# Reordering the dense jobs under the FoX attention, with an even fill and operands kept as 512-token tiles

## The chip, the cores and the metric

The kernel runs on one core of a Trainium2 chip. Its time is device microseconds, the median of the runs shown. The core has a matrix engine (PE, with its weight loads as a second row, PEld), three engines for elementwise work (VectorE, in the profile DVE; ScalarE, ACT; GpSimd, POOL) and a queue that starts transfers (SP). Each engine works through its own list of instructions in order; semaphores make one wait for another.

## The reference

One layer of a decoder trunk over 1024 tokens and 1024 channels, all in fp32. After an RMS norm, one input projection feeds eight HGRN heads and sixteen FoX heads; both groups are gated, concatenated, projected back and added to the residual. Then a per-layer embedding is gated in, and a final norm ends it.

```python
u = rmsnorm(h, norm_w[i])
proj = jnp.einsum('bsd,de->bse', u, w_in[i])
hq, hf, hi, hg, fq, fk, fv, fg, fz = jnp.split(proj, SPLIT_POINTS, axis=-1)
y_h = hgrn2_branch(hq, hf, hi, lb_all[i], hgrn_gn[i]) * jax.nn.silu(hg)
y_f = fox_branch(fq, fk, fv, fz, fox_fb[i]) * jax.nn.silu(fg)
y = jnp.concatenate([y_h, y_f], axis=-1)
h = h + jnp.einsum('bse,ed->bsd', y, w_out[i])
ple = jnp.einsum('bsk,kd->bsd', p[i], w_ple[i])
h = h + jax.nn.sigmoid(jnp.einsum('bsd,de->bse', h, w_ple_gate[i])) * ple
...
# fox_branch, per head: causal softmax of
logits = (jnp.einsum('bhtd,bhsd->bhts', qb, kb).astype(f32) * scale
          + F[:, :, q0:q1, None] - F[:, :, None, :q1])
```

## The kernel before

**Dense products.** Tokens lie along the free axis. A dense product multiplies eight 128x128 weight tiles with the normed input u. Both are split into a high and a low part (`split`, L80 and L81), and three products of parts are summed: per 128 output channels and 512 tokens that is 8 x 3 = 24 matmuls into one PSUM tile `ps`, of which there are two ("proj", pool `pp`). A dense *job* (`dense_steps`) is two such groups, 48 matmuls. u is eight tiles of 1024 tokens, high and low, each read in halves.

**FoX.** The 16 heads are worked in eight pairs. A pair p needs four jobs: q (`fox_q`), k (`fox_k`), v (`fox_v`) and a gate (`fox_gate`). Once a k or q half is out of PSUM, GpSimd makes a copy with the heads' halves swapped (`swap`, L442). For v, ScalarE copies a half to `vt` (L478), four PE transposes turn it (L483), ScalarE copies that to `v` (L485) and GpSimd swaps it. A gate writes `sg` through ScalarE (tanh, L433) and VectorE (L434); there is a single `sg` buffer and a single output buffer `o`, beside `o7` for the last pair.

A pair has four chunks: head i = 0, 1, and within it first the later 512 tokens (c = 1, wide rows of logits, 512 down to 288), then the earlier (c = 0, narrow, 256 down to 32). While a chunk is finished, the logits of the following one are begun. `Chunk.mix` does that in two parts. In each part stand 16 logit matmuls of the following chunk (L809; VectorE adds the bias and takes the extremum, L823), the exponentials of this chunk (ScalarE L845, then VectorE transposes L846), and a *fill*: `ahead.fill(FOX_FILL[p])` draws that many columns of dense work from a list of jobs, in steps of one 512-column matmul. After both parts come the maxima `mxo` (VectorE L832, L833) and the values matmuls `po` (L857), whose halves are added through `avt` (ScalarE L868) into `o` (VectorE L869). With c = 0 the row sums are turned on PE (L898), taken out by ScalarE and VectorE (`zk` L902, `zt` L903), inverted, and sent through DRAM (`zd`) to come back as `rz`, broadcast.

**What sets the order.** PE's instructions are pinned to the order in which the Python code issues them. The other engines are ordered by a list scheduler. The dense jobs issued during pair p are, before the change, v, q and k of pair p+1 and then (p from 1 to 5) the gate of p; the last pair does the gates of 6 and 7. Ahead of a pair's last chunk `until(("k", p + 1))` draws jobs until k of the next pair is done, because that chunk issues the next pair's first logits. What a job leaves to be done later (the turning of v, the row sums) is put on a list `pending` that is emptied at the third step of each group of 24 (`flush`), and at a pair's end. If a fill ends on a group's last matmul, what follows that group (its copy out of PSUM) is issued only when the next fill, or the final draining, resumes the job.

**End of FoX.** `finish` multiplies `o` by `rz` (GpSimd L916) and by `sg` (L918) and stores it. The HGRN outputs are loaded again (`y_load`: two into slots of `k`, two into `v`, four into the probabilities' tile `pt1` near the end), split into `y_h`, which takes the memory of u, and multiplied by the first half of the output weights (L96 to L98); `ev_h1` (L1000) adds the result to x.

## Time and profile before

| | |
|---|---|
| median of 3 runs | 1357.4 us (1357.19 to 1359.22) |
| the profiled execution's own time | 1359.17 us |
| its span, first to last instruction | 1357.1 us |
| PE busy | 1286.0 us (95%) |
| VectorE, ScalarE, GpSimd busy | 789.4, 473.9, 355.2 us |
| FoX, first logits to the first product with `y_h` | 548.4 to 1068.2 us |

The profiled execution has 2.1 us around its span. In the views quoted below a line of a timeline gives start, duration, engine, line, operation and, in brackets, how long the engine stood idle before it and what released it. A line of a wait view gives the waiting engine and line, what it waited for, total us, number of times and the longest. A line of a table by stage gives the stretch, its length, the busy time of PE, PEld, DVE, ACT and POOL with instruction counts, the granted PE clock, and the transfers' share and rate. A busy PE is not a PE at full speed: logits that are spaced out by a slow reader still count as busy.

### The profile page before, as it was taken

Reading aid. Unit: us, or ns where it says so; the run is one execution under the profiler, and the core shown is the slowest. Engines: PE = TensorE matmul, PEld = TensorE weight load, DVE = VectorE, ACT = ScalarE, POOL = GpSimd, SP = SyncE. Lnnn points to the kernel's source line nnn. Section 1 sums busy time; section 2 is a strip of 40 time slices with the busy share of each in tenths; the row PEclk is TensorE's granted clock in tenths of the full one; section 3 lists DMA queues with packets and bytes.
Section 4 is the critical chain, followed back from the end, with each engine's and each line's share of the span. In section 5 each row is a group of like instructions: output and inputs, shape, how many; then the busy total and the mean of one; then the engine's idle time right before and its main releaser. Section 6 shows DMA issues by size and latency. Waiting matters only on the chain. (4 is left out here: it accounts for less than half of the span.)

```text
span 1357.1 us, 26771 instructions
## 1 busy us (share of the span) xinstructions
PE 1286.0 (95%) x10996; PEld 1022.7 (75%) x10996; DVE 789.4 (58%) x1988; ACT 473.9 (35%) x1144; POOL 355.2 (26%) x288
## 2 busy tenths in 40 slices
PE   6899999999999999999999999999987899999996
PEld 4787888888888878665676767676654688888895
DVE  6746575656746574567665656565758623333465
ACT  6413122221312233443443444444434511212455
POOL 3613123112211123333332324242330300101232
PEclk9999999999999999998999999999998999999998
DMA  7312111101101012111221212121221453212312
GB/s 281 131 43 63 48 37 59 63 17 63 48 32 63 19 48 80 48 56 58 68 72 55 71 56 72 55 71 56 71 87 49 163 193 109 86 47 70 132 63 78
DMA packets 38682, 101.17 MB, mean 75 GB/s; under 512 B 6688, under 2 KB 8864, under 8 KB 38560
## 3 DMA queue, kind: packets, MB, share of 16 engines
q1 hardware_dynamic: 38416, 98.95, 22.1%
q8 instruction: 86, 1.41, 0.4%
q0 software_dynamic: 144, 0.52, 0.1%
q14 instruction: 36, 0.29, 0.1%
HBM read 82.54 MB, written 16.91 MB: 73 GB/s over the span
## 5 line engine op out<-in xcount | busy, mean ns | idle before, releaser
L356 PE MATMUL ps<-ulo,whi 128*128 128x512 f32 x896 | 359.7, 401 | 0.0
L356 PE MATMUL ps<-uhi,whi 128*128 128x512 f32 x896 | 356.8, 398 | 0.0
L356 PE MATMUL ps<-uhi,wlo 128*128 128x512 f32 x896 | 354.6, 396 | 0.0
L81 POOL TENSOR_TENSOR wlo<-wf,whi 128x1024 fp32r<-128x1024 f32 x59 | 144.7, 2453 | 496.4 <-ACT whi L80 468.1
L356 PEld LDWEIGHTS ps<-ulo,whi 128*128 128x128 f32 x896 | 169.3, 189 | 51.6 <-issue 17.6
L356 PEld LDWEIGHTS ps<-uhi,whi 128*128 128x128 f32 x896 | 169.3, 189 | 42.3 <-issue 7.4
L356 PEld LDWEIGHTS ps<-uhi,wlo 128*128 128x128 f32 x896 | 169.5, 189 | 34.8 <-issue 1.6
L845 ACT ACTIVATE x<-x,mxo 128x512 f32<-128x512 f32 (+15 forms) x256 | 130.4, 511 | 72.1 <-DVE mxo L833 72.1
L80 ACT CAST whi<-wf 128x1024 fp32r<-128x1024 f32 (+1 forms) x77 | 79.6, 1035 | 213.8 <-PE ps L97 92.5
L823 DVE CUSTOM_DVE_ANT_0 x<-lg,fb 128x512 f32<-128x512 f32 (+15 forms) x256 | 101.8, 431 | 90.2 <-PE lg L809 83.4
L846 DVE STREAM_TRANSPOSE pt<-x 128x512 f32<-128x512 f32 (+15 forms) x256 | 115.9, 459 | 40.8 <-ACT x L845 36.5
L809 PE MATMUL lg<-k,qx 64*32 64x512 f32 (+15 forms) x1024 | 83.5, 431 | 24.7 <-POOL k L442 20.3
L96 PE MATMUL ps<-yhi,whi 128*128 128x512 f32 x256 | 100.8, 394 | 5.5 <-DVE h L1000 5.5
L97 PE MATMUL ps<-ylo,whi 128*128 128x512 f32 x256 | 100.8, 394 | 0.0
L98 PE MATMUL ps<-yhi,wlo 128*128 128x512 f32 x256 | 100.6, 393 | 0.0
L809 PE MATMUL lg<-k,q 64*32 64x480 f32 (+15 forms) x1024 | 82.9, 429 | 3.8 <-DVE mx L823 3.8
L857 PEld LDWEIGHTS po<-pt,v 64*64 64x64 f32 x1536 | 53.6, 133 | 23.4 <-issue 9.4
L857 PE MATMUL po<-pt,v 64*64 64x256 f32 (+7 forms) x1536 | 69.4, 320 | 0.0
L809 PEld LDWEIGHTS lg<-k,qx 64*32 64x32 f32 x1024 | 28.9, 109 | 45.7 <-POOL k L442 22.3
L96 PEld LDWEIGHTS ps<-yhi,whi 128*128 128x128 f32 x256 | 48.7, 190 | 15.9 <-issue 5.9
L97 PEld LDWEIGHTS ps<-ylo,whi 128*128 128x128 f32 x256 | 48.8, 191 | 10.5 <-DVE ylo L81 0.2
L98 PEld LDWEIGHTS ps<-yhi,wlo 128*128 128x128 f32 x256 | 48.8, 191 | 10.3
(204 smaller groups left out, 2178.8 us busy)
## 6 DMA issues: line engine op xcount, KB each, us to landing
wf<-in_w_in_dram SPq DMA_DIRECT2D x64, 512.0 KB, 3.5
fb<-fd SPq DMA_DIRECT2D x64, 128.0 KB, 3.3
wf<-in_w_out_dram SPq DMA_DIRECT2D x16, 512.0 KB, 3.5
yf<-yd SPq DMA_DIRECT2D x16, 512.0 KB, 4.9
x<-in_xT_dram SPq DMA_DIRECT2D x8, 512.0 KB, 9.2
pled<-pleo SPq DMA_DIRECT2D x16, 256.0 KB, 3.1
yd<-sg SPq DMA_DIRECT2D x8, 512.0 KB, 2.6
rz<-zd SPq DMA_DIRECT2D x16, 256.0 KB, 3.4
```

Source lines behind the costliest of these rows:

```text
L80: pin(nc.scalar.copy(hi, src))
L81: pin(lo_engine.tensor_tensor(out=lo, in0=src, in1=hi, op=ALU.subtract))
L96: pin(mm(ps, whi, uhi, start=i == 0, stop=False))
L97: pin(mm(ps, whi, ulo, start=False, stop=False))
L98: pin(mm(ps, wlo, uhi, start=False, stop=i == n - 1))
L356: pe(mm(ps, x, y, start=i == j == 0, stop=i == n - 1 and j == 2))
L809: mm(ps[32 * j : 32 * j + 32, m % 2, : 32 * n], q[:, 32 * (j // 2) :][:, :32], k[not own][rows].rearrange("p (t a k) -> p t a k", a=2, k=3 ...
L823: nc.vector.tensor_tensor_reduce(out=x, in0=ps[:, m % 2, : 32 * n], in1=copies[m % 2][:, : 32 * n], scale=1.0, scalar=BIG, op0=ALU.add, op ...
L845: nc.scalar.activation(x, x, AF.Exp, bias=self.other[:, g : g + 1], scale=-1.0, accum_out=zs[:, m : m + 1])
L846: nc.vector.transpose(self.probs[:, : m + 1, g], x.rearrange("p (t k) -> p t k", k=32))
L857: mm(po[half[t % 2], r, 32 * first : 256], v_t[self.p][half[r], t ^ r, half[self.i]], self.probs[half[r], t, first:].rearrange("p g q -> p ...
```

## The change

Four things are done together.

1. **Order of jobs.** During pair p the jobs are now k and q of pair p+1, the gate of p (p from 1 to 4), then v of pair p+1. The weight loads (`w_in_loads`) follow that order.
2. **A gate moves.** The gate of pair 5 is no longer computed in pair 5 but at the beginning of the last pair, which then has three gates (5, 6, 7). Since `o` is needed by pair 6, the output of pair 5 is stored after its multiplication by `rz`, loaded again in the last pair as `olate` (into a `k` slot), multiplied by the gate and stored again. One of the early `y_load`s goes to a slot of `q` instead.
3. **Even fill.** FOX_FILL becomes exact multiples of 18 matmuls (9216 columns) or 24 (12288): 18 x 8 = 144 is three jobs, 24 x 8 = 192 is four. The last pair's fill goes from 8 matmuls to 18 in each part.
4. **512-token tiles.** u, `y_h` and `hm` become separate tiles for each half of the tokens, so that a half's memory is free as soon as that half has been read.

```diff
-FOX_FILL = (9200, 12300, 12300, 12300, 12300, 12300, 9200, 4000)
+FOX_FILL = (9216, 12288, 12288, 12288, 12288, 9216, 9216, 9216)
+FIRST_LATE = PAIRS_F - 3
...
-    upool = ctx.enter_context(tc.tile_pool(name="u", bufs=2 * KT))
+    upool = ctx.enter_context(tc.tile_pool(name="u", bufs=2 * KT * NCH))
...
+    def operands(*names):
+        return [[tuple(upool.tile([P, CH], F32R, name=name, tag="u") for name in names) for _ in range(KT)] for _ in range(NCH)]
...
         for p in range(PAIRS_F - 1):
-            tiles += [T_FV + p + 1, T_FQ + p + 1, T_FK + p + 1] + ([T_FG + p] if 0 < p < PAIRS_F - 2 else [])
-        tiles += [T_FG + PAIRS_F - 2, T_FG + PAIRS_F - 1]
+            tiles += [T_FK + p + 1, T_FQ + p + 1] + ([T_FG + p] if 0 < p < FIRST_LATE else []) + [T_FV + p + 1]
+        tiles += [T_FG + p for p in range(FIRST_LATE, PAIRS_F)]
...
-                    ahead.fill(FOX_FILL[self.p] if following else 5000)
+                    ahead.fill(FOX_FILL[self.p])
...
-                    ahead.jobs += [gate_late(p - 1), fox_gate(p)]
-                    for x in ((fp, "k", 4), (fp, "k", 4), (fp, "v", 2, 2)):
+                    y_t[FIRST_LATE] = fp.tile([P, S], F32, name="olate", tag="k", bufs=4)
+                    nc.sync.dma_start(out=y_t[FIRST_LATE], in_=yd[KT + FIRST_LATE])
+                    ahead.jobs += [gate_late(p - 2), gate_late(p - 1), fox_gate(p)]
+                    for x in ((fp, "k", 4), (fi, "q", 2), (fp, "v", 2, 2)):
                         y_load(*x)
...
-                    ahead.jobs += [fox_v(p + 1), fox_q(p + 1), fox_k(p + 1)]
-                    if 0 < p < PAIRS_F - 2:
+                    ahead.jobs += [fox_k(p + 1), fox_q(p + 1)]
+                    if 0 < p < FIRST_LATE:
                         ahead.jobs.append(fox_gate(p))
+                    ahead.jobs.append(fox_v(p + 1))
...
                 finish(p, False)
-                if p != PAIRS_F - 2:
+                if p == FIRST_LATE:
+                    nc.sync.dma_start(out=yd[KT + p], in_=y_t[p])
+                elif p != PAIRS_F - 2:
                     finish(p, True)
...
-        y_h = [(upool.tile([P, S], F32R, name="yhi", tag="u"), upool.tile([P, S], F32R, name="ylo", tag="u")) for _ in range(KT)]
+        y_h = operands("yhi", "ylo")
```

PE, near the end of pair 3, where its second head's row sums are turned (`zs`). Before, with gate matmuls around:

```order
L356 MATMUL ps<-uhi,wlo 128x512
L356 MATMUL ps<-uhi,whi 128x512
L898 MATMUL ps<-cst,zs 16x128
L356 MATMUL ps<-ulo,whi 128x512
L356 MATMUL ps<-uhi,wlo 128x512
```

Now, with matmuls of v of pair 4 around, and the turning of that v's first half (`vt`) right behind:

```order
L359 MATMUL ps<-uhi,wlo 128x512
L359 MATMUL ps<-uhi,whi 128x512
L900 MATMUL ps<-cst,zs 16x128
L485 MATMUL ps<-cst,vt 128x128 x4
L359 MATMUL ps<-ulo,whi 128x512
```

The transposes of `vt` write a PSUM tile of the same two-tile pool as the row sums just before them, while the other tile is being summed.

PE at the end of pair 3 itself. Before, from the last gate matmul over the values to the first logits of the next chunk:

```order
L356 MATMUL ps<-uhi,wlo 128x512
L857 MATMUL po<-pt_8010,v 64x256 x4
L857 MATMUL po<-pt_8010,v 64x192 x2
L857 MATMUL po<-pt_8010,v 64x160 x2
L857 MATMUL po<-pt_8010,v 64x128 x2
L857 MATMUL po<-pt_8010,v 64x96 x2
L857 MATMUL po<-pt_8010,v 64x64 x2
L857 MATMUL po<-pt_8010,v 64x32 x2
L809 MATMUL lg<-k,qx 32x256
```

Now, from the last matmul of v:

```order
L359 MATMUL ps<-uhi,wlo 128x512
L859 MATMUL po<-pt_7999,v 64x256 x4
L859 MATMUL po<-pt_7999,v 64x192 x2
L859 MATMUL po<-pt_7999,v 64x160 x2
L859 MATMUL po<-pt_7999,v 64x128 x2
L859 MATMUL po<-pt_7999,v 64x96 x2
L859 MATMUL po<-pt_7999,v 64x64 x2
L859 MATMUL po<-pt_7999,v 64x32 x2
L485 MATMUL ps<-cst,vt 128x128 x4
L811 MATMUL lg<-k,qx 32x256
```

Four transposes of v's second half stand between the values and the next logits; before, v's transposes stood six matmuls into a later group of dense work.

ScalarE over the same stretch of pair 3. Before:

```order
L902 COPY zk<-ps 16x64
L845 ACTIVATE x_8048,zs<-x_8048,mxo 128x512
...
L845 ACTIVATE x_8048,zs<-x_8048,mxo 128x352
L433 ACTIVATE sg<-ps 128x512
L80 CAST whi<-wf 128x1024
L845 ACTIVATE x_8048,zs<-x_8048,mxo 128x320
L845 ACTIVATE x_8048,zs<-x_8048,mxo 128x288
L868 COPY avt<-po 64x512
L478 ACTIVATE vt<-ps 128x512
```

Now:

```order
L904 COPY zk<-ps 16x64
L847 ACTIVATE x_8037,zs<-x_8037,mxo 128x512
L847 ACTIVATE x_8037,zs<-x_8037,mxo 128x480
L487 COPY v<-ps 128x4x128
L847 ACTIVATE x_8037,zs<-x_8037,mxo 128x448
...
L847 ACTIVATE x_8037,zs<-x_8037,mxo 128x320
L82 CAST whi<-wf 128x1024
L847 ACTIVATE x_8037,zs<-x_8037,mxo 128x288
L870 COPY avt<-po 64x512
L480 ACTIVATE vt<-ps 128x512
L487 COPY v<-ps 128x4x128
L467 COPY k<-ps 128x512
```

The eight exponentials are those of the next pair's first chunk. In both lists `avt` and then `vt` stand behind all eight; the `vt` of the new list is the one that PE's four transposes at the pair's end read.

More of the change, by code (lines that the diff above doesn't have):

```diff
@@ L104, in dense @@
             ps = pp.tile([P, CH], F32, name="ps", tag="proj")
-            sl = slice(c * CH, (c + 1) * CH)
-            product(ps, [(whi[:, j], wlo[:, j], mov[j][0][:, sl], mov[j][1][:, sl]) for j in range(k)])
+            product(ps, [(whi[:, j], wlo[:, j], *mov[c][j]) for j in range(k)])
             evac(c, ps)
@@ L121, in rstd @@
         pin(nc.vector.scalar_tensor_tensor(out=y, in0=t, scalar=1.5, in1=y, op0=ALU.add, op1=ALU.mult))
-    u = []
+    def operands(*names):
+        return [[tuple(upool.tile([P, CH], F32R, name=name, tag="u") for name in names) for _ in range(KT)] for _ in range(NCH)]
     wt_st = ExitStack()
@@ L142, in token_major @@
             ps = pp.tile([P, 2 * P], F32, name="ps", tag="proj")
-            sl = slice(b * P, (b + 1) * P)
-            product(ps, [(u[j][0][:, sl], u[j][1][:, sl], w[0][:, j], w[1][:, j]) for j in range(KT)])
+            sl = slice(b % 4 * P, (b % 4 + 1) * P)
+            product(ps, [(u[b // 4][j][0][:, sl], u[b // 4][j][1][:, sl], w[0][:, j], w[1][:, j]) for j in range(KT)])
             evac_pin(nc.vector.tensor_copy(out=v[:, :, b], in_=ps.rearrange("p (i d) -> p i d", i=2)))
@@ L256, in trunk @@
         rs, newt = ([sp2.tile([P, CH], F32, name=name) for _ in range(NCH)] for name in ("rstd", "newt"))
-        for i in range(KT):
-            u.append((upool.tile([P, S], F32R, name="uhi", tag="u"), upool.tile([P, S], F32R, name="ulo", tag="u")))
+        u = operands("uhi", "ulo")
         cst = const.tile([P, P + 32], F32, name="cst")
@@ L277, in u_split @@
         def u_split(k, c, lo_engine):
-            split(u[k][0][:, half[c]], u[k][1][:, half[c]], xs[k][:, half[c]], lo_engine, pin)
+            split(*u[c][k], xs[k][:, half[c]], lo_engine, pin)
         v = v0p.tile([P, 2, FB, P], F32, name="v", tag="v")
@@ L364, in dense_steps @@
             ps = pp.tile([P, CH], F32, name="ps", tag="proj")
-            sl = slice(c * CH, (c + 1) * CH)
-            yield from product_steps(ps, [(whi[:, j], wlo[:, j], mov[j][0][:, sl], mov[j][1][:, sl]) for j in range(KT)], CH)
+            yield from product_steps(ps, [(whi[:, j], wlo[:, j], *mov[c][j]) for j in range(KT)], CH)
             evac(c, ps)
@@ L408, in fox_gates @@
                 for i in range(2):
-                    pe(mm(ps[:48], wzs[:, k, :48], u[k][i][:, sl], start=k == i == 0, stop=k == KT - 1 and i == 1))
+                    pe(mm(ps[:48], wzs[:, k, :48], u[c][k][i], start=k == i == 0, stop=k == KT - 1 and i == 1))
                     yield CH
@@ L517, in steps @@
                     ps = pp.tile([P, 2 * P], F32, name="ps", tag="proj")
-                    sl = slice(b * P, (b + 1) * P)
+                    sl = slice(b % 4 * P, (b % 4 + 1) * P)
                     yield from product_steps(
-                        ps, [(u[j][0][:, sl], u[j][1][:, sl], w[0][:, j], w[1][:, j]) for j in range(KT)], 2 * P
+                        ps, [(u[b // 4][j][0][:, sl], u[b // 4][j][1][:, sl], w[0][:, j], w[1][:, j]) for j in range(KT)], 2 * P
                     )
@@ L981, in trunk @@
             for e in range(KT):
-                split(y_h[e][0][:, sl], y_h[e][1][:, sl], y_f32[e][:, sl], nc.vector)
+                split(*y_h[c][e], y_f32[e][:, sl], nc.vector)
     with ExitStack() as st:
@@ L1007, in ev @@
                 nc.vector.tensor_tensor(out=h[n][:, sl], in0=ps, in1=h[n][:, sl], op=ALU.add)
-                split(hm[n][0][:, sl], hm[n][1][:, sl], h[n][:, sl], nc.vector)
+                split(*hm[c][n], h[n][:, sl], nc.vector)
             return ev
@@ L1020, in trunk @@
         with tc.tile_pool(name="yp", bufs=2 * KT, reuse_waits="tile") as yp:
-            y_f = []
+            y_f = [[] for _ in range(NCH)]
             w = [first_w, load_w(a["w_out"][1], KT, nc.vector, tc.keep_in_program_order)]
@@ L1030, in trunk @@
                 split(hi, lo, y, nc.vector, tc.keep_in_program_order)
-                y_f.append((hi, lo))
+                for c in range(NCH):
+                    y_f[c].append(tuple(t[:, c * CH : (c + 1) * CH] for t in (hi, lo)))
             for n in range(2):
                 gw[n] = load_gate(n, g01, ("ghi", "glo"), tag="g")
-            hm = [(upool.tile([P, S], F32R, name="hh", tag="u"), upool.tile([P, S], F32R, name="hl", tag="u")) for _ in range(KT)]
+            hm = operands("hh", "hl")
             for n in range(KT):
@@ L1053, in gate @@
             ps = eps_.tile([P, w], F32, name="gps", tag="gate", bufs=4)
-            product(ps, [(whi[:, j], wlo[:, j], hm[j][0][:, sl], hm[j][1][:, sl]) for j in range(KT)])
+            own = slice(t0 - c * CH, t1 - c * CH)
+            product(ps, [(whi[:, j], wlo[:, j], *(t[:, own] for t in hm[c][j])) for j in range(KT)])
             g = gp.tile([P, w], F32, name="g", bufs=2)
@@ L1057, in gate @@
             nc.vector.scalar_tensor_tensor(
-                out=g, in0=g, scalar=1.0, in1=pl[n][:, t0 - c * CH : t1 - c * CH], op0=ALU.add, op1=ALU.mult
+                out=g, in0=g, scalar=1.0, in1=pl[n][:, own], op0=ALU.add, op1=ALU.mult
             )
```

## The prediction

> **What bounds the kernel now.** I read the page's busy times first, then PE's waits, then PE's timeline around the long ones, and last the granted clock by stage.
>
> ```profile
> PE 1286.0 (95%) x10996; PEld 1022.7 (75%) x10996; DVE 789.4 (58%) x1988; ACT 473.9 (35%) x1144; POOL 355.2 (26%) x288
> ```
>
> PE is the bound: 71.1 us of the span are left for it. No other engine comes near, so what counts is where PE waits.
>
> ```profile
> PE lg L809 <- POOL k L442: 20.3, 7, 4.8
> PE lg L809 <- DVE mx L823: 8.1, 8, 2.1
> PE ps L96 <- DVE h L1000: 5.5, 1, 5.5
> PE ps L898 <- ACT v L485: 1.4, 2, 0.7
> ```
>
> Three of these belong to the change: logits wait seven times for the swapped k of the next pair, they wait for VectorE, and the first product with `y_h` waits once at the end of FoX. The seven are the pair ends, and I take them as milestones:
>
> ```profile
> 613.74 1.06 PE L809 MATMUL lg<-k,qx 64*32 64x512 f32 x1 [4.80 <-POOL k L442]
> 672.14 0.61 PE L809 MATMUL lg<-k,qx 64*32 64x512 f32 x1 [2.14 <-POOL k L442]
> 738.31 0.61 PE L809 MATMUL lg<-k,qx 64*32 64x512 f32 x1 [2.14 <-POOL k L442]
> 806.08 0.61 PE L809 MATMUL lg<-k,qx 64*32 64x512 f32 x1 [2.14 <-POOL k L442]
> 872.25 1.02 PE L809 MATMUL lg<-k,qx 64*32 64x512 f32 x1 [2.14 <-POOL k L442]
> 940.05 0.61 PE L809 MATMUL lg<-k,qx 64*32 64x512 f32 x1 [2.14 <-POOL k L442]
> 1011.87 0.70 PE L809 MATMUL lg<-k,qx 64*32 64x512 f32 x1 [4.80 <-POOL k L442]
> 1068.16 0.39 PE L96 MATMUL ps<-yhi,whi 128*128 128x512 f32 x1
> ```
>
> The stretches between them last 58.4, 66.2, 67.8, 66.2, 67.8, 71.8 and 56.3 us. Why equal pairs differ by 1.6 shows in the clock of the first 8 us or so of a stretch:
>
> ```profile
> 672.20:680.00 7.80, 7.80 (x72) 5.20 (x80) 2.91 (x10) 0.54 (x1) 1.24 (x1) 1.00 0.15 60
> 738.40:746.00 7.60, 7.60 (x51) 4.76 (x52) 2.91 (x10) 0.00 (x0) 1.21 (x1) 0.78 0.15 59
> 806.10:814.00 7.90, 7.90 (x72) 5.29 (x80) 2.91 (x10) 0.60 (x1) 1.27 (x1) 1.00 0.16 62
> 872.30:880.00 7.70, 7.70 (x51) 4.47 (x52) 2.91 (x10) 0.00 (x0) 1.24 (x1) 0.78 0.14 54
> 940.10:948.00 7.90, 7.90 (x52) 4.83 (x53) 2.91 (x10) 0.00 (x0) 1.25 (x1) 0.78 0.15 58
> 1020.00:1068.00 48.00, 40.74 (x450) 28.36 (x450) 40.24 (x131) 27.23 (x85) 4.87 (x3) 0.93 0.29 102
> 1085.00:1091.00 6.00, 6.00 (x15) 4.70 (x16) 2.52 (x3) 0.00 (x0) 0.00 (x0) 0.52 0.80 249
> 1090.00:1300.00 210.00, 210.00 (x948) 174.82 (x947) 76.61 (x91) 55.53 (x71) 19.57 (x8) 1.00 0.31 100
> ```
>
> After a wait of 2.14 us the clock falls in three of five cases (0.78 over 7.6 us, that is 0.22 x 7.6 = 1.7 us lost), and after the 5.5 us at the end to 0.52 over 6.0 us, 2.9 lost. A stretch of four jobs without either takes 66.2 - 2.1 = **64.0 us**. The cost of a job:
>
> ```profile
> 1062.47 0.39 PE L356 MATMUL ps<-uhi,wlo 128*128 128x512 f32 x1
> 1067.93 0.39 PE L356 MATMUL ps<-uhi,wlo 128*128 128x512 f32 x1
> 552.91 0.60 PE L483 MATMUL ps<-cst,vt 128*128 128x128 f32 x4
> ```
>
> Between the first two lie 24 steps, 5.46 / 24 = 0.2275 us each, so a job of 48 is 10.9 us. Against the ideal, the seven stretches contain: first, three jobs, 64.0 - 10.9 = 53.1; then five of four jobs, 320.0; last, two jobs, 64.0 - 2 x 10.9 = 42.2. Together 415.3, and they take 454.4. With the 4.8 in front of the first, **PE loses 43.9 us** up to the first `y_h` product: waits at pair ends 20.3; clock after them 3 x 1.7 = 5.1; the last stretch 56.3 - 42.2 = 14.1; and 4.4 in the two stretches that begin or end with a 4.8 us wait and its crowded logits.
>
> **The change part by part.**
>
> *Keys first.* k of the next pair is ready two parts into a pair, its swap four parts ahead of the logits that read it. The 20.3 go, the 5.1 and the 4.4 with them: 29.8 us removed. Nothing is added to PE's matmuls.
>
> *Values last.* v now ends exactly on the pair's last fill, so its second half is copied out of PSUM and turned only when the pair is drained. The four transposes stand in PE's list right behind the pair's values, and wait for `vt`, which stands in ScalarE's list behind `avt`, and that behind the eight wide exponentials of the next chunk. Queued behind the waiting transposes is everything on PE: the next logits and fills, and with them VectorE. The end of pair 3 gives the sizes, PE's two rows, VectorE's two and ScalarE's five:
>
> ```profile
> 814.86 0.50 PE L356 MATMUL ps<-ulo,whi 128*128 128x512 f32 x1
> 820.42 1.31 PE L857 MATMUL po<-pt,v 64*64 64x256 f32 x32
> 814.03 0.69 DVE L434 SCALAR_TENSOR_TENSOR sg<-sg,ps 128x512 f32<-128x512 f32 x1 [3.63 <-ACT sg L433]
> 817.91 0.20 DVE L903 TENSOR_TENSOR zt<-ps,zk 16x64 f32<-16x64 f32 x1
> 818.08 0.72 ACT L845 ACTIVATE x<-x,mxo 128x512 f32<-128x512 f32 x1 [1.22 <-DVE mxo L833]
> 821.93 0.58 ACT L433 ACTIVATE sg<-ps 128x512 f32<-128x512 f32 x1
> 822.41 1.04 ACT L80 CAST whi<-wf 128x1024 fp32r<-128x1024 f32 x1
> 824.54 0.58 ACT L868 COPY avt<-po 64x512 f32<-64x512 f32 x1
> 828.39 0.60 ACT L478 ACTIVATE vt<-ps 128x512 f32<-128x512 f32 x1 [3.27 <-PE ps L356]
> ```
>
> Let X be the end of the wide logits, 814.86. In the changed order of pairs 1 to 4, PE goes on with 7 matmuls (1.6) and the row sums (0.3), and would turn v's first half at X + 1.9. That needs the PSUM tile of the row sums, which VectorE frees with `zt`, here at X + 3.25; the gate's 0.69 ahead of VectorE's sums is gone at that place, so X + 2.65. **First wait 0.8.** Then transposes 0.6, 17 matmuls 3.9, values 1.3: X + 8.5. ScalarE's exponentials begin at X + 3.2, now 0.6 sooner; with the weights' cast, and a copy of v where the gate's 0.58 was, `avt` starts at X + 9.7 - 0.6 = 9.1 and `vt` ends 1.2 later; with the semaphore PE turns v at X + 10.35. **Second wait 1.85**, sum 2.65. In pairs 0, 5 and 6 the fill is 18 matmuls: 1 matmul (0.2), transposes 0.6, then the row sums wait 0.7 for ScalarE's copy of v (the wait row of `ps L898` above, 1.4 in 2), 0.3, 3.9, 1.3, X + 7.0; `vt` without the extra copy ends at X + 9.7; PE goes on at 9.8. Wait 2.8, sum 3.5. Over the pairs 4 x 2.65 + 3 x 3.5 = **21.1 us**. The bounds: if ScalarE is idle when the values end, `avt` and `vt` alone are 0.58 + 0.60 + 0.1 = 1.3, with nothing for VectorE, and the 0.7 three times: 7 x 1.3 + 2.1 = 11.2. From above the nearest row is the 4.80 at a pair end, 33.6.
>
> The clock: by the rows above a wait of 2.1 costs 1.7 in three cases of five. I take the same for each pair end, 7 x 0.6 x 1.7 = **7.1**, between 0 and 11.9.
>
> The Trainium skill ("TensorE: Matmul & The Clock Gate", section "HAM oscillation — how this bites in real kernels") says that only a PE idle gap longer than some 3.4 us slows the clock. The trace shows 0.78 after 2.14 us, so the measurement decides here; by the rule the sum would be 7.1 us better, as the third rival works out.
>
> *The gate of pair 5 in the last pair, and its fill.* Pair 5 loses a job, the last gains one: no sum changes. What changes is the cover: the last stretch is PE-poor, with 40.24 us of VectorE in 48.00 and 8 matmuls a part. PE's waits from 1020 to 1068:
>
> ```profile
> PE lg L809 <- DVE mx L823: 7.3, 6, 2.1
> ```
>
> That is 7.3 of the 8.1 us of the whole kernel. With 18 matmuls a part has 4.1 us of fill, as in pairs 0 and 6, in whose filled parts PE does not wait for `mx`. I keep **2.0** of the 14.1, between 0 (that likeness) and 14.1 (nothing gained). The reload of `olate` and its second store lie on SP between loads that have whole parts to land; GpSimd's multiplication is off PE's path as long as the single `sg` is free before the next gate's first half leaves PSUM, 24 matmuls or 5.5 us later, against 2.4 us of work. Nothing for these.
>
> *End of FoX.* The rows of GpSimd, VectorE and SP:
>
> ```profile
> 1070.45 7.47 POOL L916 TENSOR_TENSOR o<-o,rz 128x1024 f32<-128x1024 f32 x1 [8.37 <-DMA rz<-zd]
> 1077.99 2.37 POOL L918 TENSOR_TENSOR o<-o,sg 128x1024 f32<-128x1024 f32 x1
> 1070.21 4.29 DVE L81 TENSOR_TENSOR ylo<-yf,yhi 128x512 fp32r<-128x512 f32 x7
> 1074.42 1.21 DVE L81 TENSOR_TENSOR wlo<-wf,whi 128x1024 fp32r<-128x1024 f32 x1
> 1083.96 1.29 DVE L1000 TENSOR_TENSOR h<-ps,xr 128x512 f32<-128x512 f32 x2 [8.33 <-DMA yd<-o]
> 1060.20 1.31 PE L857 MATMUL po<-pt,v 64*64 64x256 f32 x32
> ```
>
> Today `h` comes 22.4 us after the last values (1061.51), and 29 + 48 matmuls cover most of it. In the new order the row sums come 17 matmuls and the values earlier, so `rz`, 10.3 us behind them (1060.2 to 1070.45), is there 5.1 after the values; GpSimd's first product takes 2.4 to 7.5, since it stands still under VectorE's splits as the row of 7.47 shows; I take 3.7, as the 512-token tiles let half of the splits go earlier. The second 2.4, the store 3.6 (1080.36 to 1083.96), `h` 0.7: 15.5. PE has 48 `y_h` matmuls, 10.9. Wait 4.6 instead of 5.5, same clock loss: **0.9** gained, between -2.9 (7.5) and 2.2 (2.4).
>
> *512-token tiles* otherwise: products read the same columns in the same order; in the 210 us from 1090 PE is busy throughout, so there is no wait to take away. Nothing.
>
> **The sum:** 43.9 - 21.1 - 7.1 - 2.0 + 0.9 = 14.6 us. The profiled execution, 1359.17 (span 1357.1 and 2.1 around it), would become 1344.6. It lies 1.8 above the median shown, so the median goes from 1357.4 to **1342.8**.
>
> **The rivals.**
>
> *Pair ends freed.* ScalarE is through its exponentials when the values end, and the waits are at their lower bound without clock loss: 43.9 - 11.2 - 2.0 + 0.9 = 31.6, **1325.8**. For it: ScalarE is busy 35%. Against: at 824.54 `avt` came 2.8 us after the values' end, behind exponentials.
>
> *The last pair keeps its loss.* Its limit would be VectorE, not want of matmuls: three gates bring VectorE another 2 x 0.69 us. Then 12.1 of the gain stay out: **1354.9**, no change. For it: 40.24 of 48.00. Against: the waits for `mx` are not there in parts with 18 matmuls.
>
> *The waits are too short for the clock.* Two waits under 3 us each, apart by 17 matmuls, leave it at 1.00 as after 672: 7.1 less, **1335.7**. For it: two of five cases. Against: the other three.
>
> *Slower.* `mxo` comes late in pairs with small fills, because VectorE's work per part stays while PE's shrinks; the exponentials then start late, `vt` later, and PE stands with all fills behind it. The point is 14.6 / 7 = 2.1 us more per pair end than worked out; at 4 more, still near the 4.80 row with its clock loss, it is 28 - 14.6 = 13.4 slower, **1370.8**. For it: the idle 1.22 of ScalarE before 818.08, waiting for `mxo`. Against: VectorE's 58% busy over the span.
>
> **How the numbers follow.** Forecast 0.48, pair ends freed 0.20, clock unharmed 0.10, last pair unchanged 0.10, slower 0.12. A measurement of this kernel tells 0.2%, 2.7 us, from no change; so faster 0.78, same 0.10, slower 0.12. The likeliest case's own range is 1336 to 1350; with the bounds of the pair ends and the last pair, 8 in 10 is 1326 to 1357.
>
> **What would show it.** Right: no wait of logits for k L442; seven new waits of PE's transposes L485 for ScalarE's `vt`, 1.8 to 2.8 each, and four of about 0.8 for `zt`; waits for `mx` under 2 us in the last pair; `h` some 4.6 late. Wrong: waits of L485 under 1.4 or over 4, granted clock below 0.9 in pairs with 18 matmuls, or a last pair longer than 56 us.

## The result, and the profile after

| | before | changed |
|---|---|---|
| median | 1358.31 us (1357.19 to 1359.59, 4 runs) | 1350.15 us (1349.51 to 1351.1, 4 runs) |
| profiled execution, span | 1357.1 us | 1349.2 us |
| PE busy | 1286.0 us | 1284.5 us |

The ratio of changed to before is 0.994, with a 95% interval of 0.9923 to 0.9957. That is 8.2 us faster by the medians; 14.6 were forecast. One execution of an experiment below (the late turn in the pairs of four jobs alone) took 3225.2 us, against 1337.42 to 1338.68 in the other three, and is left out of its median. The lines are now two further down than before (k's swap L444, `vt` L480, `v` L487, the row sums L900, `zt` L905, the products of `o` L918 and L920); from L1000 on they are seven further.

PE's waits between 540 and 1100 us in the changed kernel (waiting engine and line, what for, total us, times, longest):

```profile
PE ps L485 <- ACT vt L480: 18.8, 7, 3.9
PE ps L485 <- DVE zt L905: 4.8, 4, 1.2
PE lg L811 <- DVE mx L825: 2.5, 5, 1.0
PE ps L900 <- ACT v L487: 2.0, 3, 0.7
PE ps L98 <- DVE h L1007: 1.8, 1, 1.8
...
```

No logits wait for k any more; those 20.3 us are gone. In their place stand the seven waits of the transposes for `vt`, with two smaller kinds beside them: 25.6 us (18.8 + 4.8 + 2.0), more than was taken away. The seven, one at each pair's end, in PE's timeline:

```profile
617.65 1.11 PE L485 MATMUL ps<-cst,vt 128*128 128x128 f32 x4 [3.85 <-ACT vt L480]
687.22 0.96 PE L485 MATMUL ps<-cst,vt 128*128 128x128 f32 x4 [1.78 <-ACT vt L480]
...
1012.10 1.11 PE L485 MATMUL ps<-cst,vt 128*128 128x128 f32 x4 [3.85 <-ACT vt L480]
```

Three last 3.85 us, behind the pairs with three jobs (0, 5 and 6), and four last 1.8 us, behind the pairs with four. What the clock did in the 9 to 10 us behind each of the seven (stretch, length, busy time of PE, PEld, DVE, ACT and POOL, granted clock, transfers):

```profile
617.70:627.00 9.30, 9.30 (x60) 6.66 (x60) 1.85 (x11) 0.58 (x1) 6.08 (x6) 0.74 0.33 115
687.30:697.00 9.70, 9.70 (x94) 6.96 (x95) 2.32 (x14) 1.17 (x2) 6.80 (x7) 0.82 0.29 108
756.10:766.00 9.90, 9.90 (x102) 7.64 (x103) 3.90 (x24) 1.17 (x2) 7.91 (x8) 1.00 0.31 108
823.40:833.00 9.60, 9.60 (x94) 6.99 (x95) 2.19 (x13) 1.17 (x2) 6.69 (x7) 0.82 0.32 109
892.30:902.00 9.70, 9.70 (x101) 7.47 (x102) 4.83 (x26) 1.36 (x3) 7.62 (x8) 1.00 0.35 122
950.70:960.00 9.30, 9.30 (x87) 6.54 (x87) 1.91 (x12) 0.58 (x1) 3.74 (x5) 0.66 0.31 113
1012.10:1022.00 9.90, 9.90 (x89) 7.03 (x90) 2.44 (x16) 0.58 (x1) 3.74 (x5) 0.68 0.46 160
```

The shortfall from 1.00 times the length gives 2.4, 1.7, 0, 1.7, 0, 3.2 and 3.2: **12.2 us** of clock, on top of the waits. The row "PE busy" hides it, since a slow PE is a busy one.

The end of FoX, in the timelines: PE's first product with `y_h` and the one that waits for `h`, GpSimd's two products, VectorE's splits beside them.

```profile
1066.05 0.50 PE L98 MATMUL ps<-yhi,whi 128*128 128x512 f32 x1
...
1079.45 0.47 PE L98 MATMUL ps<-yhi,whi 128*128 128x512 f32 x1 [1.77 <-DVE h L1007]
```

```profile
1069.31 2.86 POOL L918 TENSOR_TENSOR o<-o,rz 128x1024 f32<-128x1024 f32 x1 [13.56 <-DVE o L871]
1072.25 2.73 POOL L920 TENSOR_TENSOR o<-o,sg 128x1024 f32<-128x1024 f32 x1
```

```profile
1069.20 7.53 DVE L83 TENSOR_TENSOR ylo<-yf,yhi 128x512 fp32r<-128x512 f32 x5
```

and the stretch behind that wait for `h`:

```profile
1079.40:1091.00 11.60, 11.55 (x51) 9.58 (x52) 3.80 (x5) 0.70 (x2) 0.00 (x0) 1.00 0.88 328
```

PE came to `y_h` only 2.1 us sooner than before (1068.16). The rest of the gain was made behind that: the wait for `h` is 1.77 us instead of 5.46, and the clock behind it stays at 1.00, where 0.52 was granted before from 1085 to 1091.

### The profile page after: what moved, and what is told of

Its sections match the earlier page's. It is cut to its first block, busy times and chain, and to the rows that moved or that the text cites. A ratio compares the mean times of both kernels' runs of the same rounds, so it can differ in the third digit from the quotient of the medians.

```text
span 1349.2 us, 26805 instructions
## 1 busy us (share of the span) xinstructions
PE 1284.5 (95%) x10996; PEld 1024.2 (76%) x10996; DVE 794.6 (59%) x1988; ACT 475.2 (35%) x1144; POOL 350.4 (26%) x288
## 4 chain that ended last, share of the span: by engine, by line
PE 78%; DVE 10%; ACT 7%; issue 2%; DMA 2%; POOL 1%; SPq 0%; DVEq 0%; ACTq 0%; POOLq 0%
PE ps L359 45%; PE lg L811 5%; PE ps L98 4%; PE ps L100 4%; PE ps L99 4%; PE po L859 4%; ACT x L847 3%; DVE x L825 2%; PE ps L566 1%; PE gps L98 1%; PE gps L99 1%; PE gps L100 1%; DVE x L275 1%; PE po L707 1%; PE po L709 1%
## 5 line engine op out<-in xcount | busy, mean ns | idle before, releaser
L359 PE MATMUL ps<-uhi,whi 128*128 128x512 f32 x896 | 362.8, 405 | 0.0
L359 PE MATMUL ps<-ulo,whi 128*128 128x512 f32 x896 | 355.3, 397 | 0.0
L359 PEld LDWEIGHTS ps<-uhi,whi 128*128 128x128 f32 x896 | 169.7, 189 | 60.3 <-issue 25.9
L811 PE MATMUL lg<-k,q 64*32 64x480 f32 (+15 forms) x1024 | 77.7, 411 | 2.5 <-DVE mx L825 2.5
L811 PE MATMUL lg<-k,qx 64*32 64x512 f32 (+15 forms) x1024 | 78.2, 413 | 0.0
L98 PEld LDWEIGHTS ps<-yhi,whi 128*128 128x128 f32 x256 | 48.0, 188 | 12.2 <-ACT whi L82 2.2
L359 PE MATMUL ps<-wthi,uhi 128*128 128x256 f32 x192 | 54.0, 281 | 0.0
```

Of the source, the lines that this page charges most:

```text
L98: pin(mm(ps, whi, uhi, start=i == 0, stop=False))
L359: pe(mm(ps, x, y, start=i == j == 0, stop=i == n - 1 and j == 2))
L811: mm(ps[32 * j : 32 * j + 32, m % 2, : 32 * n], q[:, 32 * (j // 2) :][:, :32], k[not own][rows].rearrange("p (t a k) -> p t a k", a=2, k=3 ...
```

## The experiments

The theory after this reading (A): the change removed the waits for k, but put as much back as waits for `vt` and as clock behind them, because the turning of v's second half stands at the pair's end while `vt` stands behind eight exponentials. Against it: that any freed time at a pair end only moves to the next wait (B). The experiments first move and remove that wait, then take the change apart, then go after what is left. Each ratio is against the kernel before, run beside it on the same chip, with its 95% interval.

### The turn of v moved off the pair's end

```diff
             if i == 1 and c == 0:
-                ahead.fill()
-                ahead.flush()
+                if p == PAIRS_F - 1:
+                    ahead.fill()
+                    ahead.flush()
                 finish(p, False)
```

> The changed kernel (1350.2 us) with one edit: at the end of the pairs 0 to 6, v's second half is not turned at once behind the values but in the next pair's first fill, after its seventh product. Theory A, the seven waits for `vt` at the pair ends (18.8 us together in the changed kernel) and the lower clock behind them (up to 13.6 us by the sums over its windows) are what ate the gain: no wait of L485 for `vt` over 0.3 us, clock 0.97 or more at the pair ends, time 1318 to 1326 us. Rival B, the wait only moves: TensorE comes to the next logits or values as much too early and waits there for the exponentials or the maxima, time 1345 to 1351 us. Between the two: the waits go but the clock stays low, because the `zt` and `v` waits are still there: 1331 us.

Measured: **1323.59 us** (1322.65 to 1324.34), ratio 0.9743 (0.9729 to 0.9758). PE's waits from 540 to 1100 us:

```profile
PE ps L485 <- DVE zt L905: 4.8, 4, 1.2
PE ps L485 <- ACT vt L480: 3.5, 3, 1.2
...
PE ps L900 <- ACT v L487: 2.0, 3, 0.7
...
```

and the table by stage behind the end of pair 0:

```profile
617.70:630.00 12.30, 12.30 (x118) 9.44 (x120) 7.02 (x33) 5.74 (x20) 7.12 (x7) 1.00 0.42 130
```

A holds, B falls. Waits for `vt` go from 18.8 to 3.5 us (15.3 gained), and the clock is 1.00 throughout, with the waits of up to 1.24 us at the turns still there. 15.3 + 12.2 is 27.5, as much as the span fell by (1349.2 to 1321.7); the medians fell by 26.6. The one point where A was wrong: the three waits of 1.16 us for `vt` were to be under 0.3.

### The price of the long and of the short waits apart

As before, but the late turn only in the pairs of four jobs:

```diff
-                if p == PAIRS_F - 1:
+                if p in (0, 5, 6, 7):
                     ahead.fill()
                     ahead.flush()
```

> The changed kernel (1350.2 us) with v's second half turned late, as in e1_turn_later, in the four pairs of four jobs alone (1 to 4); the three pairs of three jobs (0, 5 and 6) keep their turn at the pair's end and their waits of 3.85 us. It tells the price of the two kinds apart. Theory A, a wait of 3.85 us costs itself and 3.4 us of clock each time, a wait of 1.8 us itself and 1.7 us of clock in two of four: four short ones gone give 7.2 + 3.4 = 10.6 us, time 1338 to 1341 us, and the three long ones stand for the rest of e1's gain, 16 us. Rival B, short waits cost the clock as much as long ones (e1's 26.6 us split evenly over seven pair ends, 3.8 each): four gone give 15.2 us, time 1335 us. Rival C, only gaps over 3.4 us slow the clock: four gone give 7.2 us alone, 1343 us.

Measured: **1337.73 us** (the three executions named above), ratio 0.9844 (0.9824 to 0.9864). The clock behind the three waits of 3.86 us that stay:

```profile
617.70:630.00 12.30, 12.30 (x102) 9.04 (x103) 3.83 (x23) 1.17 (x2) 7.31 (x8) 0.78 0.26 87
940.00:952.00 12.00, 12.00 (x104) 8.81 (x104) 5.22 (x26) 1.67 (x4) 4.91 (x7) 0.86 0.34 114
1000.00:1012.00 12.00, 12.00 (x100) 8.80 (x101) 4.80 (x27) 1.19 (x2) 3.73 (x5) 0.77 0.36 132
```

Four short waits gone are worth 12.4 us against the 1350.15 of the changed kernel, by the medians and by the spans (1349.2 and 1336.8). The waits are 7.2 of it. Of the 5.2 left, 3.4 are the clock behind two of the four in the changed kernel; and the three long waits cost less clock here, 2.7 + 1.7 + 2.8 = 7.2 instead of 8.8, which is 1.6 more. The time lies 0.3 under the range of A (1338 to 1341), 2.7 above B (1335) and 5.3 below C (1343), by which short waits leave the clock alone. The rows speak for A in the price of a short wait and against it in that of a long one, which is 1.7 to 2.8 of clock here and not 3.4 each time. By the spans the three long waits stand for the other 15.1 us of the first experiment: 3 x (3.86 - 1.16) = 8.1 of waiting and 7.2 of clock.

### The wait's cause taken away instead

Fills one column longer, so that v's copy is issued ahead of the values, and ScalarE held to the order of the program for `vt` and the exponentials:

```diff
-FOX_FILL = (9216, 12288, 12288, 12288, 12288, 9216, 9216, 9216)
+FOX_FILL = (9217, 12289, 12289, 12289, 12289, 9217, 9217, 9217)
...
-            nc.scalar.activation(vt, ps, AF.Copy, scale=0.5)
+            pe(nc.scalar.activation(vt, ps, AF.Copy, scale=0.5))
...
-                nc.scalar.activation(x, x, AF.Exp, bias=self.other[:, g : g + 1], scale=-1.0, accum_out=zs[:, m : m + 1])
+                pe(nc.scalar.activation(x, x, AF.Exp, bias=self.other[:, g : g + 1], scale=-1.0, accum_out=zs[:, m : m + 1]))
```

> The changed kernel (1350.2 us) with the wait left where it is and its cause taken away in another way: the fills of a pair end one column later, so that v's last product and its copy `vt` come ahead of the values in the program, and ScalarE's copies `vt` and the exponentials keep the order of the program, so that `vt` is no longer behind eight exponentials of the next chunk. Theory A, ScalarE's order makes the 18.8 us: no wait of L485 for `vt` over 1 us, time 1321 to 1332 us, unless the fixed order makes the exponentials later. Rival B, the exponentials are needed first: kept behind `vt` and behind the values' copies they come late, TensorE waits for the probabilities or the maxima, and the time is 1345 us or more.

Measured: **1324.25 us** (1323.9 to 1324.73), ratio 0.9746 (0.9732 to 0.9761). PE's waits from 540 to 1100 us:

```profile
PE ps L98 <- DVE h L1007: 5.9, 1, 5.9
...
PE ps L485 <- ACT vt L480: 2.2, 5, 1.3
```

PE's first product with `y_h`, GpSimd's first product behind the returned row sums, and the stage at the end of FoX:

```profile
1033.69 0.50 PE L98 MATMUL ps<-yhi,whi 128*128 128x512 f32 x1 [0.82 <-DVE sg L436]
```

```profile
1039.70 2.97 POOL L918 TENSOR_TENSOR o<-o,rz 128x1024 f32<-128x1024 f32 x1 [15.96 <-DMA rz<-zd]
```

```profile
1040.00:1060.00 20.00, 14.06 (x55) 11.16 (x54) 8.00 (x7) 1.99 (x2) 6.66 (x3) 0.83 0.58 212
```

A holds, but for one of the five waits for `vt` that are left, 1.33 us in pair 0, where it had none over 1. It is a second way to the same cause and to nearly the same gain: it was ScalarE's order that made the wait. It shows a limit too. PE is at `y_h` 32.4 us sooner than in the changed kernel, but only 25.9 arrive: `rz` lands 6 us behind that point, `h` is waited for 5.94 us, and the clock falls, to a mean of 0.83 over these 20 us.

### Tiles of 1024 tokens again

```diff
...
-        return [[tuple(upool.tile([P, CH], F32R, name=name, tag="u") for name in names) for _ in range(KT)] for _ in range(NCH)]
+        full = [tuple(upool.tile([P, S], F32R, name=name, tag="u") for name in names) for _ in range(KT)]
+        return [[tuple(t[:, c * CH : (c + 1) * CH] for t in full[k]) for k in range(KT)] for c in range(NCH)]
```

> The changed kernel (1350.2 us) with the moving operands in 1024-token tiles again, every instruction the same. Theory A, the smaller tiles let the first product that needs a new residual start sooner at the end of FoX: the wait of L98 for `h` goes back from 1.77 us to about 5.5 us and the clock behind it to about 0.72, and the time rises by about 6.6 us to 1356.8 us. Rival B, the end of FoX gained from the order of the jobs and the gates: wait for `h` stays at about 1.8 us, time 1350 us within 1.5 us.

Measured: **1349.48 us**, ratio 0.9932 (0.9915 to 0.9948). PE's wait for `h`, and GpSimd's product in the timeline:

```profile
PE ps L98 <- DVE h L1008: 1.7, 1, 1.7
```

```profile
1069.71 2.93 POOL L919 TENSOR_TENSOR o<-o,rz 128x1024 f32<-128x1024 f32 x1 [13.44 <-DVE o L872]
```

B holds. The tiles do nothing here, at the end of FoX as elsewhere. The gain there came from the rest of the change.

### The gate back in pair 5

Job order, fills of pairs 0 to 4 and tiles as changed:

```diff
-FOX_FILL = (9216, 12288, 12288, 12288, 12288, 9216, 9216, 9216)
+FOX_FILL = (9216, 12288, 12288, 12288, 12288, 12288, 9216, 4000)
-FIRST_LATE = PAIRS_F - 3
+FIRST_LATE = PAIRS_F - 2
...
-                    ahead.fill(FOX_FILL[self.p])
+                    ahead.fill(FOX_FILL[self.p] if following else 5000)
...
```

> The changed kernel (1350.2 us) with the gate of pair 5 back in pair 5 and the fills of the last pairs as before (12288, 9216, 4000 and 5000 at the last chunk); job order, the other fills and tiles as changed. Theory A, the last pair had too little to do and the gate filled it: pair 5 ends with the shorter `vt` wait (1.8 us instead of 3.85 us, and some 1.7 us less lost to the clock), the last pair loses some 12 us again, time 1358 to 1361 us. Rival B, the last pair's loss was only put off to the end of FoX: time 1350 us within 2 us.

Measured: **1352.42 us** (1350.95 to 1353.43), ratio 0.9955 (0.994 to 0.997): 2.3 us over the changed kernel, with intervals that overlap. Pair 6's end and the first product with `y_h`:

```profile
1019.21 1.12 PE L485 MATMUL ps<-cst,vt 128*128 128x128 f32 x4 [3.86 <-ACT vt L480]
...
1068.65 0.39 PE L98 MATMUL ps<-yhi,whi 128*128 128x512 f32 x1
```

A is refuted, and the time lies 0.4 above the range of B. The last pair does lose: it lasts 49.4 us for two jobs, where the changed kernel takes 54.0 for three, so its third job (10.9) cost the changed kernel only 4.5 there, and 6.4 were regained. But pair 6's end comes only 7.1 us later than in the changed kernel (1012.10), though a whole job was put ahead of it: with four jobs again, pair 5 ends with the short wait, 3.8 us cheaper. The net is 2.6 up to the first product with `y_h`. Behind that point, as B had it, this is made up: PE meets no wait for `h` there, and the profiled spans are 1349.1 and 1349.2. So the 2.3 between the medians are not shown to be the gate's.

### The gate move alone, and the order alone

The kernel before with the gate move and the fills that go with it (9200 in pair 5, 9216 in the last) alone:

```diff
...
-            tiles += [T_FV + p + 1, T_FQ + p + 1, T_FK + p + 1] + ([T_FG + p] if 0 < p < PAIRS_F - 2 else [])
-        tiles += [T_FG + PAIRS_F - 2, T_FG + PAIRS_F - 1]
+            tiles += [T_FV + p + 1, T_FQ + p + 1, T_FK + p + 1] + ([T_FG + p] if 0 < p < FIRST_LATE else [])
+        tiles += [T_FG + p for p in range(FIRST_LATE, PAIRS_F)]
...
```

> The kernel before (1358.3 us) with only the gate of pair 5 moved to the last pair and the last pair's fill made 9216 columns; order of the jobs (values, queries, keys), other fills and 1024-token tiles as before. Theory A, the gate move alone gives the last pair's 12 us, less some 1 us for the shorter pair 5: time 1345 to 1348 us, which is less than the whole change has, so that order and fill together cost time. Rival B, the gate move is worth nothing without the new order: 1356 to 1360 us.

The kernel before with the new order of the jobs alone, its old fills (12300, 9200) kept:

```diff
...
-                    ahead.jobs += [fox_v(p + 1), fox_q(p + 1), fox_k(p + 1)]
+                    ahead.jobs += [fox_k(p + 1), fox_q(p + 1)]
                     if 0 < p < PAIRS_F - 2:
                         ahead.jobs.append(fox_gate(p))
+                    ahead.jobs.append(fox_v(p + 1))
```

> The kernel before (1357.6 us) with only the new order of the jobs (keys, queries, gate, values); fills, gates and tiles as before. Theory A, the order alone makes what the gate's return (e4_gate_back, 1352.4 us) left of the gain, and the even fills and tiles make nothing: 1351 to 1354 us, with waits for `vt` of 16 to 19 us. Rival B, the uneven fills (12300, 9200) end v's last product a product sooner and so let `vt` be issued ahead of the exponentials: waits for `vt` under 10 us, time 1340 to 1346 us.

Measured: the gate alone **1352.25 us**, ratio 0.9953 (0.9939 to 0.9968); the order alone **1353.9 us**, ratio 0.9963 (0.995 to 0.9977). PE's waits from 540 to 1100 us with the gate alone:

```profile
PE lg L811 <- POOL k L444: 22.9, 7, 4.8
PE lg L811 <- DVE mx L825: 4.8, 6, 1.2
PE ps L98 <- DVE h L1006: 2.5, 1, 2.5
...
```

and with the order alone, with GpSimd's product at the end of FoX from its timeline:

```profile
PE ps L898 <- ACT v L485: 12.8, 7, 2.3
PE ps L483 <- ACT vt L478: 7.7, 2, 3.9
PE ps L96 <- DVE h L1001: 5.5, 1, 5.5
PE lg L809 <- DVE mx L823: 4.5, 5, 1.8
```

```profile
1065.53 7.24 POOL L916 TENSOR_TENSOR o<-o,rz 128x1024 f32<-128x1024 f32 x1 [9.32 <-DMA rz<-zd]
```

Either alone gives about 5 us and both with the even fills 8.2: less than the two together, but the intervals allow a plain sum as well. The gate alone stands between its theories: the waits for `mx` shrink (8.1 to 4.8), and so does that for `h` (5.46 to 2.5), but pair 5, now of three jobs, waits 4.8 for k instead of 2.1. The order alone has the time that A gave, and waits like B's: with the old fills `vt` is waited for only twice, 7.7 us, but the row sums wait 2.3 us five times for `v`. That is 20.5 us in sum, against 21.7 before (20.3 for k, 1.4 for v): the order by itself turns one wait into another of the same size. What it gains is at the last pair and behind it: `mx` is waited for 4.5 us instead of 8.1, and PE meets the same wait for `h` 5.1 us sooner (1079.67 us instead of 1084.80). Of these 5.1, 2.0 were there ahead of FoX: in this execution the first logits start at 546.33 instead of 548.37.

### What is left: the two steps set apart

The first experiment, with the two delayed steps, the row sums and half a `v`, no longer at one place but after the seventh and the sixteenth product:

```diff
-                if i == 2 and j == 0:
-                    ahead.flush()
+                if i in (2, 5) and j == 0 and ahead.pending:
+                    ahead.pending.pop(0)()
```

> The kernel of e1_turn_later (1323.6 us) with its two delayed steps in a fill (the row sums' turn and the turn of half of v) set apart: one after the seventh product, one after the sixteenth, so that the second no longer finds the PSUM tile of the first still in use. Theory A, the ten waits of 0.67 to 1.24 us left at these places (10.3 us together: `zt` 4.8, `vt` 3.5, `v` 2.0) are waits for a PSUM tile and for ScalarE that nine products (2.1 us) cover: they go below 1.5 us in sum, no clock is lost by waits that short, so only they are gained: 1313 to 1316 us. Rival B, the steps later in the fill delay the exponentials' sums, `rz` and the values, so that as much is waited for elsewhere: 1322 to 1325 us.

and after the thirteenth and the twenty-second:

```diff
-                if i in (2, 5) and j == 0 and ahead.pending:
+                if i in (4, 7) and j == 0 and ahead.pending:
```

> The kernel of e7_spaced (1320.0 us) with the two delayed steps after the thirteenth and the twenty-second product of a run instead of the seventh and the sixteenth. In e7_spaced seven waits for `vt` are left, three of 1.54 us and four of 0.46 us (6.5 us): `vt` stands in ScalarE's order behind the exponentials and is only then done. Theory A, six products (1.36 us) of cover take the four away and leave 0.2 us of the three: 1313.5 to 1316 us. Rival B, the values of the next chunk, which need this half of v, or the row sums' way to `rz` are late instead: 1319 us or more.

Measured: **1319.98 us**, ratio 0.9713 (0.9699 to 0.9728), and **1314.41 us**, ratio 0.9677 (0.966 to 0.9695). PE's one kind of wait left at the turns in the first of them, and the longest kind from 540 to 1100 us in the second:

```profile
PE ps L485 <- ACT vt L480: 6.5, 7, 1.5
```

```profile
PE ps L98 <- DVE h L1008: 1.7, 1, 1.7
...
```

The first missed both theories. The waits for a PSUM tile (`zt` 4.8, `v` 2.0) went, but those for `vt` grew from 3.5 to 6.5: of 10.3 us only 3.8 were gained, and 3.6 show. PE came sooner to a `vt` that was no sooner done. With six products more of cover this too is gone, as A had it: no wait for `vt` is left in the second kernel, and its time lies in the range of A.

### The products at the end of FoX

The last pair's two products of `o` on VectorE instead of GpSimd, first alone in the kernel before, then in the last kernel above:

```diff
-                nc.gpsimd.tensor_tensor(out=o, in0=o, in1=rz_t.pop(p), op=ALU.mult)
+                (nc.vector if p == PAIRS_F - 1 else nc.gpsimd).tensor_tensor(out=o, in0=o, in1=rz_t.pop(p), op=ALU.mult)
...
-                nc.gpsimd.tensor_tensor(out=o, in0=o, in1=sg_t[p], op=ALU.mult)
+                (nc.vector if p == PAIRS_F - 1 else nc.gpsimd).tensor_tensor(out=o, in0=o, in1=sg_t[p], op=ALU.mult)
```

> The kernel before (1358.3 us) with the two products at the end of FoX (`o` by `rz`, `o` by the gate, last pair only) on VectorE instead of GpSimd, where they took 7.47 and 2.37 us beside VectorE's splits. Theory A, GpSimd's stretched product makes `h` late: `h` comes some 7 us sooner (9.84 less two of 1.2 us and a split between), the wait of 5.46 us and the 2.9 us of clock behind it go, 1350 to 1352 us. Rival B, VectorE now waits for `rz` (which landed at 1070.45 us) with its splits queued behind, and the first products with `y_h` are late by what `h` gains: 1356 to 1360 us.

> The kernel of e10_spaced_later with the last pair's two products on VectorE as in e11_last_on_vector. There GpSimd's two take 2.86 and 2.73 us and VectorE's splits beside them are stretched by 4.4 us; `h` is late by 1.77 us. Theory A: `h` comes 2.6 us sooner, its wait and the 0.4 us for `ylo` go, 2 us less than e10_spaced_later, 1312 to 1314 us if that comes out as expected. Rival B: VectorE waits for `rz` and the splits behind it are late: no gain, or up to 2 us more.

Measured alone: **1354.83 us**, ratio 0.9972 (0.9956 to 0.9988), between the theories. The wait for `h` is gone; the wait of this line is in its place:

```profile
1074.38 0.50 PE L97 MATMUL ps<-ylo,whi 128*128 128x512 f32 x1 [2.28 <-DVE ylo L81]
```

Both theories are partly right: `h` is in time, and VectorE's splits behind the products are late.

With the other edits: **1311.47 us** (1309.79 to 1312.77), ratio 0.9654 (0.9632 to 0.9676), the fastest here, 46 us below the kernel before and 39 below the changed one. The first of VectorE's two products there (1.22 us each), and all that PE waits for from 540 to 1100 us:

```profile
1032.66 1.22 DVE L918 TENSOR_TENSOR o<-o,rz 128x1024 f32<-128x1024 f32 x1
...
```

```profile
PE lg L811 <- DVE mx L825: 1.1, 2, 0.8
PE po L859 <- POOL v L444: 0.5, 1, 0.5
```

The waits for `h` and `ylo` (2.0 us) are gone, as A had it; the time is 0.5 under its range. The intervals of this kernel and of the one without this edit overlap, but the four times of each do not (1309.79 to 1312.77, against 1313.72 to 1315.31): that it gains is shown, the size of 2.9 us only roughly.

## Why the prediction was right or wrong

The direction was right, and so was the order of the causes: new waits for `vt` and the clock behind them took back most of what the keys' order freed. The time of 1350.15 lies in the range of 1326 to 1357, at the very edge of the likeliest case's own (1336 to 1350); the gain is 8.2 us instead of 14.6. Part of that is luck: the pair ends came out far worse than worked out, and 5.7 us more than forecast at the end of FoX hide half of it. By the terms of the sum:

- **Removed, 43.9 us to begin with.** Right as to the waits for k: none is left. Up to the first product with `y_h` the forecast was 43.9 - 21.1 - 7.1 - 2.0 = 13.7 us gained; 2.1 were. The 43.9 were about right in sum, but not in their parts: PE's waits are 29.7 us of it and the clock 13.2, not 5.1. The clock fell behind the two waits of 4.80 us as well, and twice in the last pair:

```profile
613.70:620.00 6.30, 6.18 (x68) 1.40 (x72) 3.84 (x13) 0.00 (x0) 0.00 (x0) 0.52 0.20 77
1011.90:1043.10 31.20, 25.24 (x319) 13.83 (x320) 25.90 (x95) 10.28 (x36) 2.50 (x2) 0.84 0.16 59
```

  So the clock alone gave little: 13.2 us of it before, 12.2 after.
- **Waits at the pair ends: 21.1 forecast, 25.6 measured.** The pairs of four jobs came out as worked out for the second wait (1.8 against 1.85) and longer for the first (1.2 against 0.8). The step that failed is the one in the three-job pairs, "wait 2.8", which is 3.85. The exponentials were to begin 2.6 us behind the wide logits (3.2 less 0.6) in both kinds of pairs. The dense matmul behind the logits and the first exponential, at the end of pair 0 and of pair 3:

```profile
606.77 0.51 PE L359 MATMUL ps<-uhi,whi 128*128 128x512 f32 x1
610.42 0.72 ACT L847 ACTIVATE x<-x,mxo 128x512 f32<-128x512 f32 x1 [1.51 <-DVE mxo L835]
...
812.57 0.50 PE L359 MATMUL ps<-uhi,whi 128*128 128x512 f32 x1
815.62 0.72 ACT L847 ACTIVATE x<-x,mxo 128x512 f32<-128x512 f32 x1 [0.81 <-DVE mxo L835]
```

  They begin 3.65 us behind in pair 0 and 3.05 in pair 3. So the 0.6 us that the gate's absence was to give VectorE came to 0.15; this 0.45 is in both kinds of pairs, and in those of four jobs it is also what makes the first wait 1.2 instead of 0.8. VectorE's rows at these two ends, and GpSimd's row at pair 0's end, show most of the 0.6 that the three-job pairs lose besides:

```profile
608.76 1.23 DVE L834 COPY mxo<-mx 32x8 f32<-32x8 f32 x4
...
814.57 0.69 DVE L834 COPY mxo<-mx 32x8 f32<-32x8 f32 x4
```

```profile
608.50 1.29 POOL L444 TENSOR_SCALAR v<-v 64x512 f32<-64x512 f32 x2 [8.84 <-ACT v L487]
```

  Where GpSimd swaps v beside it, VectorE's copy of the extrema takes 1.23 us instead of 0.69. It is the same at 1003.22 us, beside GpSimd's swap at 1002.95. That the swap is the cause is read from the rows; no run took it away.
- **Clock: 7.1 forecast, 12.2 measured.** The mechanism was right, the size was not. A price of 1.7 us in 0.6 of the cases came from waits of 2.14 us; the 1.8 us waits did cost 1.7 us in two of four, but the 3.85 us ones cost 2.4, 3.2 and 3.2, every time. Which of the short waits cost it goes mostly by their place in time, as the last section shows, and the sum had no means to know that. Taking away the turn at the pair ends gave back the waits and the 12.2 almost to the microsecond.
- **The last pair: 2.0 kept of 14.1.** What is left is 1.24 us of waits for `mx` (the rest of its loss is the clock behind pair 6's end, counted above), so the term held. But the gate was credited with the whole difference. With the gate put back and the rest kept, 6.4 us return in the last pair, 3.8 are saved at pair 5's end, and the 2.6 between them are made up behind FoX. A pair made shorter by a job ends with the longer wait, and the sum priced that at 0.85 us (3.5 against 2.65).
- **End of FoX: 0.9 forecast, 6.6 measured** (3.7 of the wait, 2.9 of the clock). `rz` was there when `o` was: GpSimd began 3.2 us behind the values (1069.31 less 1066.12), not 5.1, and its two products took 2.86 and 2.73 us, not 3.7 and 2.4. So PE waits 1.77 instead of 4.6, and behind this wait the clock stayed at 1.00. Of the 6.6, 5.8 show in the spans behind the first `y_h` product (288.9 and 283.1). The reason given for the 3.7, the smaller tiles, is refuted: with wide tiles the product takes 2.93.
- **What does not add up.** Waits at the pair ends (4.5) and clock (5.1) explain 9.6 of the 11.6 us missing up to the first `y_h` product, and waits for `mx` 0.5 more (2.5 in all pairs together, where the sum had 2.0 for the last alone); 1.5 stay unassigned. Counted over this stretch, waits went from 29.7 to 28.1 us and clock from 13.2 to 12.2: the change moved the loss more than it removed it.

Of the rivals, the freed pair ends (1325.8) are not what the change does, but the first experiment made them real at 1323.6. That the last pair keeps its loss is refuted by the 1.24 us of waits for `mx` that are left there, of 7.3. The slower case did not come, but its mechanism, `mxo` and with it the exponentials late, is the one that the pair ends missed, at 0.45 and 1.05 us instead of its 2.1 and more. The rival by which such waits are too short for the clock is refuted for waits of 1.8 us and more. That rested on the rule of the Trainium skill ("TensorE: Matmul & The Clock Gate", section "HAM oscillation — how this bites in real kernels") that only PE idle gaps above some 3.4 us slow the clock; the trace disagrees, with 0.82 behind two waits of 1.8 us.

## What to carry to other kernels

When an operation is moved to the last place of a loop's round, look at what its consumer stands behind on every engine: here four transposes of 0.6 us, put at a place where their input was queued behind eight exponentials, cost nearly as much as the wait that the move removed (18.8 us against 20.3), with about as much clock behind it (12.2 us against 13.2). Price a wait of PE together with the clock behind it, and look first for a place later in PE's own list, among work that doesn't depend on it; moving the turn by one fill was worth more than three times the whole change. Where several edits attack one stretch, don't count on their gains to add: the gate and the order gave about 5 us each and 8 together, though the intervals here can't exclude 10.

## What the runs showed of the hardware that was not expected

- **The clock and the length of a wait.** In the three kernels with the turn moved off all seven pair ends and GpSimd's products kept (1323.6, 1320.0 and 1314.4 us), PE's waits of up to 1.77 us between 540 and 1100 us left the granted clock at 1.00 wherever they stood. Those of 1.8 us brought it down in two of four cases in the changed kernel, those of 3.85 us in all six cases of this kernel and of the one that keeps the long waits, by 1.7 to 3.2 us of loss. Whether a wait of 1.8 us does it can't be told from its length: the pair ends with 1.00 and 0.82 have waits of 1.78 to 1.81 us alike.
- **The clock changes on a grid of its own.** In the clock record of these traces it is 1.00 or 0.50 within FoX, and a low stretch lasts 3.41 or 6.83 us. In the changed kernel the low stretches begin at 615.75, 687.43, 823.97, 950.26 and 1011.70 us, which are 21, 40, 37 and 18 times 3.413 apart: they lie on a grid of points 3.413 us apart. This grid sorts most of the equal waits. Before, the three waits of 2.14 us that fell wholly between two grid points (738.31, 872.25, 940.05) lowered the clock, and the two that a grid point cuts (672.14, 806.08) did not. Of the 1.8 us waits in the changed kernel the one that is cut (756.05) did not, and of the three uncut ones two did; why the third (892.19) did not stays open, and no run shifted a wait on purpose.
- **VectorE and GpSimd hold each other up, and which of them pays changes.** At the end of FoX GpSimd's product took 7.47 us before while seven of VectorE's splits took 4.29 (0.61 each); in the changed kernel the product took 2.86 and five splits 7.53, where 3.05 would be five times 0.61. The rows look like turns, not like a shared rate: before, the product ended at 1077.92, 2.3 us behind VectorE's last instruction (1075.63), and the second product, with no split beside it, takes 2.37; in the changed kernel two of the five splits take 2.9 us, and the other three 0.7. Why GpSimd waited for eight VectorE instructions before and for one after was not found.
